# Two of the four attention query projections of a hybrid decoder step computed as one pair of block products

## The chip, the cores and the metric

The kernel is one program on one core of a Trainium2 chip. The metric is the device time of one execution in microseconds (us): the median of three runs is 831.8 us (830.59 to 834.57). One of the executions was profiled, and all durations below are from it.

## What is computed

One inference step of one layer. A prompt of 1024 tokens and 8 sequences of 4 sample tokens each (32 columns) go through a conditioned RMS norm, and the normed rows h are multiplied by one wide matrix w_in, whose columns feed everything else. Cut to what matters here:

```python
h, gate = adaln_in(x, c, w_ada, b_ada, g_norm)
(mq, mk, mv, mi, mf, mo, mz, aq, ak, av, az, gm, ga) = split_in(h @ w_in)
y_m, C, n, m = mlstm_branch(mq, mk, mv, mi, mf, mo, mz, C0, n0, m0, b_i, b_f, g_mn)
q = partial_rope(aq.reshape(B, T, A_HEADS, A_HEAD_DIM), pos)     # 8 query heads, 64 wide
o = attn_prompt(q, k, v, sinks)                                  # window 128, one sink a head
y_a = o.astype(x.dtype) * jax.nn.silu(az)
u = jax.nn.sigmoid(gm) * (y_m @ w_mo) + jax.nn.sigmoid(ga) * (y_a @ w_ao)
x = x + gate * (u @ w_o)
```

The query part aq is 512 columns of w_in: four "query jobs" of 128 columns (two heads each). Each gives a 128 x 1056 result (1024 prompt columns and 32 sample columns).

## The kernel before, in words

All float32 products on TensorE are made of two parts that TensorE multiplies at one column per step: operand = high + low, and high x high, high x low and low x high are summed. So each logical product is three matmuls.

**Plain jobs.** `job` (L569) computes 128 columns of w_in against all 1056 columns of h, in three pieces of 384, 384 and 288 columns (`piece`, L523). Each piece is 8 blocks of the contraction times three matmuls; a job is 72 matmuls. Behind the start, where ak and av are made, eight plain jobs run in this order (L1593 to L1597): aq0 to aq3 (`queries`, L895), mq0, mk0, mv0, mq1 (`head_jobs`). The evacuation of a query piece turns it (`rope`, L769: one shuffle, two products with tables, one sum on VectorE), stores it in qD in DRAM, and for the third piece adds the sample columns into `qpad`.

**Pairs.** The other projections come two at a time (`Pair`, L1366; `block_products`, L1516): two jobs of 128 columns are one 2 x 2 block product with seven block products instead of eight (Winograd's form of Strassen's scheme), each of 4 blocks of the contraction x 3 matmuls of 512 columns: 84 matmuls for a pair. The sums of blocks of h that it needs (t1 to t4) are formed once by `sum_blocks` (L1328): t2, t3 and t4 beside the plain jobs, t1 when they end, since it takes the place of a block that the plain jobs read. The first pair runs its products in the order 1, 6, 2, 7, (1 of the next), 5, 3, 4, so that t1 is wanted late; each later pair in the order 5, 6, 2, 7, (1 of the next), 3, 4. The weights are summed and split two products ahead (`split_ahead`), loaded with `load`, which is emitted at product 5 of the pair before (6 for the first), and the 32 sample columns are a small product of their own (`samples`, `samples_end`), emitted behind product 2 of the pair before (7 for the first). There are 18 pairs (L2011): four `head_in` (mk1 mv1, mq2 mk2, mv2 mq3, mk3 mv3), eight `gate`, two `query_gate`, four `head_gate`.

**Side work.** Everything else is emitted between the matmuls by a planner (`Side`, L113). Its clock `side.now` counts the TensorE time of the products emitted so far. A task is a Python generator: it emits some instructions and yields (lag, banks), and is taken up again when the clock has gone on by the lag and its PSUM banks have been left alone for their hold (a 2.0, b 2.0, o 4.0, and 6.0 us with a "+"). Streams (L266) bound how many tasks run at once: "m" 2 (the gates, then the four mLSTM heads), "a" 5 with 8 us between starts (the prompt attention units, four for each query job, `unit`, L826), "x" (`sum_blocks`), "s" 1 (`sample_attention`, L911, then four sample heads), "g" 1 (`ada_gate`, then `out_weights`). `head_jobs` lowers "a" to 3 when the last plain job starts (L1024) and finishes stream "g" there (L1022). A unit loads queries, keys and values, and 12 us later by the clock does scores (tile sc), then exponentials, transposes (pt), the product with the values (oT) and a store in oD. `head(h)` (L1038) loads q, k and v of one mLSTM head, and 11 us later goes through three groups of chunks.

**What is waited for.** `hook` (L2013) holds a product back by letting the clock run on: product 6 of pair 0 until t2 is formed, product 5 until t1 is, product 6 of a `query_gate` pair until all 16 units are emitted and sample attention is done, product 6 of `head_gate` h until the sample heads are done up to h (they finish in twos).

**Order on the engines.** TensorE executes in the order of emission. The other engines get an order from the framework's scheduler, which may put an instruction ahead of others emitted before it, a DMA issue above all, as soon as its buffer and its source are there by the scheduler's reckoning. All loads and most stores are issued by SyncE in one queue (`issue`, L258), which waits at the head for that DMA's buffer or source. A pool of 50 buffers of 128 x 512 ("half", `ht`, L194) serves nearly all tiles; 24 of them hold t2, t3 and t4 during the pairs. Raw weights have nine buffers (tag "wr"), split weights four and four.

Of the kernel before, what the change touches and what calls it, by code (L numbers as in the profile page):

```python
# [15 lines left out]
ALU = mybir.AluOpType  # L16
# [7 lines left out]
NT = 4  # L24
# [149 lines left out]
def body(tc, a):  # L174
    nc = tc.nc
    with ExitStack() as ctx:
# [17 lines left out]
        def ht(shape, name, dt=F32):  # L194
            return sp.tile(shape, dt, tag="half", bufs=50, name=name)
# [6 lines left out]
        def no_sync(ins, others):  # L202
            for o in others:
                tc.add_manual_dep(ins, o.name, mybir.DependencyInfo(
                    mybir.DependencyClass.NoSync, mybir.DependencyReason.DATA), reason="order of the work")
# [38 lines left out]
        def store(out, in_):  # L244
            due.append((side.now + 8.0, out, in_))
# [8 lines left out]
        def dma(out, in_, late=False):  # L254
            stores(in_.tensor)
            issue(out, in_, late)

        def issue(out, in_, late=False, eng=None):  # L258
            ins = (eng or nc.sync).dma_start(out, in_)  # L259
            ins = getattr(ins, "ins", ins)  # L260
            if late:
                no_sync(ins, free)
                free.clear()
            free.append(ins)
# [645 lines left out]

        def sample_attention():  # L911
            qpad, vns, kTs = at["qpad"], at["vns"], at["kTs"]
            kc, vc = ([ht([128, 4, 128], f"{n}{u}") for u in range(2)] for n in ("kc", "vc"))
            smask = ht([128, 2, WIN + NS], "smask")
            sinkr = cp.tile([128, 1], F32, name="sinkr")
            for u in range(2):
                dma(kc[u], a["cache_k"][:, 4 * u:4 * u + 4])
                dma(vc[u], a["cache_v"][:, 4 * u:4 * u + 4])
            dma(smask, a["smask"])
            dma(sinkr, a["sink_rows"])  # L920
            yield 12.0, "b"
            for u in range(2):
                tq = pb([128, 4, 128], f"kctp{u}")
                for j in range(4):
                    tr(tq[:, j], kc[u][:, j], ident)
                S.copy(kc[u], tq)
                yield 3.0, "b" if u == 0 else "o"
            sc = po([128, 2, WIN + NS], "scs")
            for u in range(2):
                for w in range(4):  # L930
                    b = u * 4 + w
                    qb = qpad[:, b].rearrange("p k g t -> p (k g t)")
                    r = slice(32 * w, 32 * w + 32)
                    mm(sc[r, u, 0:WIN], qb, kc[u][:, w], start=True, stop=True)
                    mm(sc[r, u, WIN:], qb, kTs, start=True, stop=True)
            p = ht([128, 2, WIN + NS], "ps")
            mx = cp.tile([128, 2], F32, name="mxs")
            for u in range(2):
                V.tensor_tensor_reduce(p[:, u], sc[:, u], smask[:, u], 1.0, sinkr, ALU.add, ALU.max,
                                       accum_out=mx[:, u:u + 1])  # L940
            nmx = cp.tile([128, 4], F32, name="nmxs")
            V.tensor_scalar(nmx[:, 0:2], mx, -1.0, None, op0=ALU.mult)
            V.tensor_scalar(nmx[:, 2:4], nmx[:, 0:2], sinkr, None, op0=ALU.add)
            den = cp.tile([128, 2], F32, name="dens")
            for u in range(2):
                S.activation(p[:, u], p[:, u], AF.Exp, bias=nmx[:, u:u + 1], accum_out=den[:, u:u + 1])
            S.activation(nmx[:, 2:4], nmx[:, 2:4], AF.Exp)
            V.tensor_tensor(den, den, nmx[:, 2:4], op=ALU.add)
            V.reciprocal(den, den)
            for u in range(2):  # L950
                V.tensor_scalar(p[:, u], p[:, u], den[:, u:u + 1], None, op0=ALU.mult)
            yield 10.0, "b"
            pt = pb([128, 4, 128], "pts")
            for u in range(2):
                tr(pt[:, u], p[:, u, 0:WIN], ident)
                tr(pt[:NS, 2 + u], p[:, u, WIN:], ident)
            pT = kc[0]
            S.copy(pT[:, 0:2], pt[:, 0:2])
            V.tensor_copy(pT[:NS, 2:4], pt[:NS, 2:4])
            yield 7.0, "o"  # L960
            o = po([128, 2, 128], "os")
            for u in range(2):
                for w in range(4):
                    r = slice(32 * w, 32 * w + 32)
                    mm(o[r, u], pT[:, u, r], vc[u][:, w], start=True, stop=False, share=4)
                for w in range(4):
                    r = slice(32 * w, 32 * w + 32)
                    mm(o[r, u], pT[:NS, 2 + u, r], vns, start=False, stop=True, share=4)
            S.copy(p[:, :, 0:128], o)
            yield 4.0, "b"  # L970
            ot = pb([128, 2, 128], "ost")
            for u in range(2):
                tr(ot[:, u], p[:, u, 0:128], ident)
            for u in range(2):
                v4 = lambda t: t.rearrange("p (w k g t) -> p w k g t", k=2, g=4, t=NT)
                for kv, r in enumerate(half_rows):
                    V.tensor_copy(osm[r, :, 16 * u:16 * u + 16].rearrange("p g (w t) -> p w g t", t=NT), v4(ot[r, u])[:, :, kv])
            samples_done.append("a")


        yhD = [dp.tile([128, SEQ], F32, name=f"yhD{h}") for h in range(NH)]
# [54 lines left out]
        mD = [[dp.tile([128, SEQ], F32, name=f"{n}D{h}") for n in "qkv"] for h in range(NH)]  # L1036

        def head(h):  # L1038
            an, wend, dec, fl = st["an"], st["wend"], st["dec"], st["fl"]
            C = [None]  # L1040
            w_ = {}
# [324 lines left out]
        class Pair:  # L1366
# [12 lines left out]
            def samples(self):  # L1379
                acc = pb([128, 128], "smp")  # L1380
                for k in range(4):
                    for j in range(4):
                        mm(acc[32 * j:32 * j + 32], c32[:, 4 * (j % 2) + k], self.raw[j // 2, j % 2][:, k],
                           start=(k == 0), stop=(k == 3), share=4)
                self.sums = ht([128, 128], "smps")
                S.copy(self.sums, acc)
# [41 lines left out]
        def ahead(self, key, src, th):  # L1428
            self.held[key] = o = ht([128, 512], "ho")
            dma(o, src[:, HALF[th]])  # L1430

        class head_in:
            names = lambda i: paired[i]
            ahead = lambda self, i: None

            def evac(self, c, th, *src):
                n, h = self.names[c]
                scale = float(128 ** -0.5) if n == "mq" else 1.0
                t = ht([128, 512], "mkv")
                if len(src) == 2:  # L1440
                    V.tensor_tensor(t, src[0], src[1], op=ALU.add)
                    src = (t,)
                if len(src) == 1 and (src[0] is not t or n == "mq"):
                    S.activation(t, src[0], AF.Copy, scale=scale)
                issue(mD[h]["mq mk mv".split().index(n)][:, HALF[th]], t, eng=nc.scalar)
                head_part(h, 1)
# [143 lines left out]
                    W = filled(pg, "bw", X, j)  # L1590
                side.tick()

        order += [("ak", 0), ("av", 0)] + [("aq", g) for g in range(4)]  # L1593
        inner = [(n, h) for h in range(NH) for n in ("mq", "mk", "mv")]
        paired = list(zip(inner[4::2], inner[5::2]))
        order += inner[:4]
# [332 lines left out]
        side.add("m", gates(gp, zg, gbias), "")  # L1929
        side.add("a", kv_turn(), "b")  # L1930
        V.on = S.on = False

        gbD, gsD = dp.tile([1, D], F32, name="gbD"), dp.tile([NS, D], F32, name="gsD")

# [73 lines left out]
                    summed("t4", k, b21, t2, ALU.subtract)  # L2008
                    yield 2.4, ""

        pairs = [Pair(head_in, i) for i in range(len(paired))] + [Pair(gate, d) for d in range(KT)] + [Pair(query_gate, i) for i in range(2)] + [Pair(head_gate, h) for h in range(NH)]  # L2011

        def hook(n, i):  # L2013
            if n == 0 and i in (6, 5):
                side.until(lambda: {6: "t2", 5: "t1"}[i] in formed)
            if i == 6:
                if pairs[n].kind is query_gate:
                    side.until(lambda: len(units_done) == 16)
                side.until(lambda: len(samples_done) >= {head_in: 0, gate: 0, query_gate: 1, head_gate: pairs[n].i + 2}[pairs[n].kind])
            if (n, i) == (OUT_WEIGHTS, 6):  # L2020
                side.add("g", out_weights())
            if (n, i) in LOADS:
                side.add("x", att_sums(LOADS.index((n, i))))
            if n == len(pairs) - 1:
                next(att, None)

        OUT_WEIGHTS = 5
        LOADS = [(len(pairs) - 2, 7), (len(pairs) - 1, 5)]
        work = block_products(pairs, hook)
        att = att_products()  # L2030
        side.add("g", ada_gate())
        side.add("x", sum_blocks())
        blocks["t1"] = block(0, 1)
        for g in range(4):
            queries(g)
        side.add("s", sample_attention(), "b")
        for h in range(NH):
            head_jobs(h)

# [337 lines left out]
```

## Time and profile before

| what | us |
|---|---|
| median of three runs | 831.8 |
| the profiled execution's own time | 830.97 |
| its span, first to last instruction | 829.2 |
| TensorE's first matmul starts | 6.45 |
| ak and av jobs (start) | 25.1 to 62.7 |
| eight plain jobs and their side work | 63.8 to 204.6 |
| 18 pairs, first matmul of the first to the last pair's sample matmuls | 204.6 to 617.4 |
| products of w_m_out | 688.4 to 734.5 |

TensorE (PE) is busy for 98% of the span, VectorE (DVE) for 71%, ScalarE (ACT) for 51%. The granted clock is 0.996 on average. In the listings, a group "out<-in" names the tiles written and read; x96 is the number of instructions; times of a matmul include its way through the array, so consecutive starts, not durations, give the rate. "SPq" is the queue of DMA issues.

### The profile page before, as it was taken

The page shows a single profiled execution, that of the slowest core. Times are in us where ns is not written, and L with a number is a line of the kernel's source. Part 1 is how long each engine was busy: PE and PEld are TensorE (multiplying, and loading weights), DVE is VectorE, ACT ScalarE, POOL GpSimd, SP SyncE. Part 2 cuts the span into 40 slices and gives each one's busy share as a digit, 9 for nine tenths or more (in the row PEclk, how much of TensorE's full clock was granted, in tenths as well). Part 3 has the DMA queues.
Part 4 walks back from the last instruction along what each step waited for, and adds up shares of the span by engine and source line. Part 5 has one row for each costly group of instructions (what it writes and reads, how often), then busy time and mean ns, then how long its engine had stood idle before and what let it go on. Part 6 is the DMA issues. An engine that isn't in the chain of part 4 may idle for free. (4 is left out here: it accounts for less than half of the span.)

```text
span 829.2 us, 15039 instructions
## 1 busy us (share of the span) xinstructions
PE 810.1 (98%) x5129; PEld 670.8 (81%) x5129; DVE 592.7 (71%) x1479; ACT 420.6 (51%) x1030; POOL 67.5 (8%) x128
## 2 busy tenths in 40 slices
PE   6999999999999999999899999999999999999996
PEld 3779897888788788888788878888888789987775
DVE  4889886647556456475567786797669988964776
ACT  5664365565474564555455454554446654334343
POOL 0120000000000001000001010000002104250000
PEclk9999999999999999999999999999999999999999
DMA  9997756346435324468756354464336785543533
GB/s 332 379 359 239 200 186 212 118 151 219 141 111 186 118 81 150 139 242 279 256 191 211 105 169 150 147 205 142 103 120 197 228 295 186 191 146 123 202 109 108
DMA packets 106689, 153.96 MB, mean 186 GB/s; under 512 B 20448, under 2 KB 54368, under 8 KB 106580
## 3 DMA queue, kind: packets, MB, share of 16 engines
q1 hardware_dynamic: 100964, 142.25, 52.2%
q10 hardware_dynamic: 4176, 6.56, 2.2%
q0 software_dynamic: 1472, 4.20, 1.4%
q8 instruction: 40, 0.66, 0.3%
q14 instruction: 37, 0.30, 0.1%
HBM read 109.22 MB, written 44.75 MB: 186 GB/s over the span
## 5 line engine op out<-in xcount | busy, mean ns | idle before, releaser
L220 ACT ACTIVATE p<-p,nmx 128x256 f32<-128x256 f32 (+1 forms) x64 | 31.0, 485 | 12.4 <-DVE nmx L220 12.1
L271 PE MATMUL g_aq<-h_h,wh_aq 128*128 128x384 f32 (+1 forms) x96 | 32.2, 336 | 0.0
L271 PE MATMUL g_aq<-h_h,wl_aq 128*128 128x384 f32 (+1 forms) x96 | 30.9, 322 | 0.0
L271 PE MATMUL g_aq<-h_l,wh_aq 128*128 128x384 f32 (+1 forms) x96 | 30.8, 321 | 0.0
L271 PE MATMUL g_w_mo<-ym_l,wh_w_mo 128*128 128x384 f32 (+1 forms) x96 | 30.8, 321 | 0.0
L271 PE MATMUL g_w_mo<-ym_h,wh_w_mo 128*128 128x384 f32 (+1 forms) x96 | 30.8, 321 | 0.0
L271 PE MATMUL g_w_mo<-ym_l,wl_w_mo 128*128 128x384 f32 (+1 forms) x96 | 30.8, 321 | 0.0
L220 DVE CUSTOM_DVE_ANT_0 p<-sc,cst,sink 128x256 f32<-128x256 f32 (+1 forms) x64 | 26.2, 464 | 5.3 <-PE sc L271 5.2
L259 POOL DMA_DIRECT2D oD<-uqv x16 | 8.9, 554 | 183.2 <-ACT uqv L220 161.0
L220 DVE COPY p<-pt 128x512 f32<-128x512 f32 (+1 forms) x16 | 10.5, 656 | 13.6 <-PE pt L276 13.6
L271 PEld LDWEIGHTS g_aq<-h_h,wh_aq 128*128 128x128 f32 x96 | 18.0, 188 | 2.5 <-issue 1.5
L271 PEld LDWEIGHTS g_w_mo<-ym_l,wh_w_mo 128*128 128x128 f32 x96 | 18.0, 188 | 0.0
L271 PEld LDWEIGHTS g_aq<-h_l,wh_aq 128*128 128x128 f32 x96 | 18.0, 188 | 0.0
L271 PEld LDWEIGHTS g_w_mo<-ym_h,wh_w_mo 128*128 128x128 f32 x96 | 18.0, 188 | 0.0
L271 PE MATMUL sc<-ukv,uqv 64*128 64x256 f32 (+1 forms) x128 | 18.0, 390 | 0.0
L271 PEld LDWEIGHTS g_w_mo<-ym_l,wl_w_mo 128*128 128x128 f32 x96 | 18.0, 188 | 0.0
L271 PEld LDWEIGHTS g_aq<-h_h,wl_aq 128*128 128x128 f32 x96 | 18.0, 188 | 0.0
L220 ACT ACTIVATE p<-p,den 128x256 f32<-128x256 f32 (+1 forms) x32 | 14.5, 491 | 5.7 <-DVE den L220 5.6
L220 DVE TENSOR_TENSOR et<-et,S 128x384 f32<-128x384 f32 (+1 forms) x12 | 6.1, 510 | 15.6 <-PE S L271 12.9
L220 ACT ACTIVATE sq<-rows_h 128x512 f32<-128x512 f32 (+2 forms) x14 | 8.2, 582 | 17.8 <-issue 12.0
L271 PE MATMUL g_mq<-h_h,wh_mq 128*128 128x384 f32 (+1 forms) x48 | 16.8, 349 | 0.3 <-ACT mk L220 0.3
L276 PE MATMUL pt<-cst,p 128*128 128x128 f32 x120 | 16.4, 277 | 0.5 <-DVE mx L220 0.5
(2073 smaller groups left out, 2842.4 us busy)
## 6 DMA issues: line engine op xcount, KB each, us to landing
x<-xT SPq DMA_DIRECT2D x16, 256.0 KB, 5.4
early_h<-w_ada SPq DMA_DIRECT2D x8, 512.0 KB, 9.0
adar_ga<-w_ada SPq DMA_DIRECT2D x16, 256.0 KB, 3.9
wr_ga<-w SPq DMA_DIRECT2D x16, 256.0 KB, 2.9
wr_gm<-w SPq DMA_DIRECT2D x16, 256.0 KB, 3.0
taD<-gt SPq DMA_DIRECT2D x16, 256.0 KB, 2.0
tmD<-gt SPq DMA_DIRECT2D x16, 256.0 KB, 5.5
wor<-w_out SPq DMA_DIRECT2D x16, 256.0 KB, 4.9
```

What stands on the lines that cost most here:

```text
L220: ins = f(*args, **kw)
L259: ins = (eng or nc.sync).dma_start(out, in_)
L271: in_order(nc.tensor.matmul(out, lhsT, rhs, start=start, stop=stop, skip_group_check=more))
L276: in_order(nc.tensor.transpose(out, in_, idn))
```

## The change

- The third and fourth query jobs leave the plain jobs and become pair 0, of a new kind `att_in`, ahead of the four `head_in` pairs. Six plain jobs and 19 pairs are left. Its `evac` sums the two parts where there are two, turns the 512 columns (shuffle, two scaled products with tables of their own, a sum), stores them in qD, and adds the four units of a query job when both halves of it are there. Its tables are loaded at product 6 (`ahead`), four of 128 x 512 and a small one.
- Its `samples` writes the sample columns of both jobs into `qpad` and starts sample attention. That first waits until four units are done, bounds the units at once to two while it runs (three afterwards), and loads the cached values later.
- A head waits until the gates are done and t1 is formed.
- While `paced` is set (from the end of the start to the first product of the last pair but one), each DMA that goes through SyncE's queue gets an ordering edge, without a semaphore, to the last TensorE instruction emitted before it.
- `out_weights` starts at pair 8 instead of 5. As the list of pairs has one more at its head, that is two pairs later in the work.

```diff
+        paced = []
+
         def issue(out, in_, late=False, eng=None):
             ins = (eng or nc.sync).dma_start(out, in_)
             ins = getattr(ins, "ins", ins)
+            if eng is None and paced:
+                no_sync(ins, [last["PE"]])
...
         def sample_attention():
             qpad, vns, kTs = at["qpad"], at["vns"], at["kTs"]
-            kc, vc = ([ht([128, 4, 128], f"{n}{u}") for u in range(2)] for n in ("kc", "vc"))
+            while len(units_done) < 4:
+                yield 1.0, ""
+            side.streams["a"]["max"] = 2
+            kc = [ht([128, 4, 128], f"kc{u}") for u in range(2)]
...
+            vc = [ht([128, 4, 128], f"vc{u}") for u in range(2)]
+            for u in range(2):
+                dma(vc[u], a["cache_v"][:, 4 * u:4 * u + 4])
             yield 10.0, "b"
...
             samples_done.append("a")
+            side.streams["a"]["max"] = 3
...
         def head(h):
+            while not st or "t1" not in formed:
+                yield 1.0, ""
...
+        class att_in:
+            names = lambda i: (("aq", 2 * i), ("aq", 2 * i + 1))
+
+            def ahead(self, i):
+                if i == 6:
+                    tables.extend([ht([128, 512], f"turn{th}{j}") for j in range(2)] for th in range(2))
+                    at["turn"] = ht([128, 2, NS], "turns")
+                    dma(at["turn"], a["rope"][:, :, SEQ:T])
+                    for th in range(2):
+                        for j in range(2):
+                            dma(tables[th][j], a["rope"][:, j, HALF[th]])
+
+            def evac(self, c, th, *src):
+                g = 2 * self.i + c
+                x, t = ht([128, 512], "aq"), ht([128, 512], "aqr")
+                if len(src) == 2:
+                    V.tensor_tensor(x, src[0], src[1], op=ALU.add)
+                else:
+                    S.copy(x, src[0])
+                V.stream_shuffle(t, x, shuf)
+                for y, f in zip((x, t), tables[th]):
+                    V.scalar_tensor_tensor(y, y, 0.125, f, op0=ALU.mult, op1=ALU.mult)
+                V.tensor_tensor(x, x, t, op=ALU.add)
+                store(qD[g][:, HALF[th]], x)
+                self.held[c] = self.held.get(c, 0) + 1
+                if self.held[c] == 2:
+                    for b0 in (0, 2, 4, 6):
+                        side.add("a", unit(g, b0))
+
+            def samples(self, o):
+                x, t = sm([128, 2, NS], "gts", 2), sm([128, 2, NS], "gts", 2)
+                S.activation(x, o, AF.Copy, scale=0.125)
+                V.stream_shuffle(t, x, shuf)
+                for y, j in ((x, 0), (t, 1)):
+                    V.tensor_tensor(y, y, at["turn"][:, j:j + 1].to_broadcast((128, 2, NS)), op=ALU.mult)
+                v3 = lambda y, r, c: y[r, c].rearrange("p (b t) -> p b t", t=NT)
+                for c in range(2):
+                    for kv, r in enumerate(half_rows):
+                        V.tensor_tensor(at["qpad"][r, :, kv, 2 * self.i + c], v3(x, r, c), v3(t, r, c), op=ALU.add)
+                side.add("s", sample_attention(), "b")
...
-        order += [("ak", 0), ("av", 0)] + [("aq", g) for g in range(4)]
+        order += [("ak", 0), ("av", 0)] + [("aq", g) for g in range(2)]
...
+        paced.append(True)
...
-        pairs = [Pair(head_in, i) for i in range(len(paired))] + ...
+        pairs = [Pair(att_in, 1)] + [Pair(head_in, i) for i in range(len(paired))] + ...
...
+            if n == len(pairs) - 2:
+                paced.clear()
-        OUT_WEIGHTS = 5
+        OUT_WEIGHTS = 8
...
-        for g in range(4):
+        for g in range(2):
             queries(g)
-        side.add("s", sample_attention(), "b")
```

More of the change, by code (lines that the diff above doesn't have):

```diff
@@ L917, in sample_attention @@
                 dma(kc[u], a["cache_k"][:, 4 * u:4 * u + 4])
-                dma(vc[u], a["cache_v"][:, 4 * u:4 * u + 4])
             dma(smask, a["smask"])
@@ L1430, in ahead @@
             dma(o, src[:, HALF[th]])
+        class att_in:
[35 more added lines that the diff above has]
+                side.add("s", sample_attention(), "b")
+        tables = []
         class head_in:
@@ L2009, in out_weights @@
                     yield 2.4, ""
-        pairs = [Pair(head_in, i) for i in range(len(paired))] + [Pair(gate, d) for d in range(KT)] + [Pair(query_gate, i) for i in range(2)] + [Pair(head_gate, h) for h in range(NH)]
+        pairs = [Pair(att_in, 1)] + [Pair(head_in, i) for i in range(len(paired))] + [Pair(gate, d) for d in range(KT)] + [Pair(query_gate, i) for i in range(2)] + [Pair(head_gate, h) for h in range(NH)]
         def hook(n, i):
@@ L2018, in hook @@
                     side.until(lambda: len(units_done) == 16)
-                side.until(lambda: len(samples_done) >= {head_in: 0, gate: 0, query_gate: 1, head_gate: pairs[n].i + 2}[pairs[n].kind])
+                side.until(lambda: len(samples_done) >= {att_in: 0, head_in: 0, gate: 0, query_gate: 1, head_gate: pairs[n].i + 2}[pairs[n].kind])
             if (n, i) == (OUT_WEIGHTS, 6):
```

## The prediction

> **What bounds the kernel now.** I read the page first: shares, span and clock.
>
> ```profile
> span 829.2 us, 15039 instructions
> PE 810.1 (98%) x5129; PEld 670.8 (81%) x5129; DVE 592.7 (71%) x1479; ACT 420.6 (51%) x1030; POOL 67.5 (8%) x128
> PEclk9999999999999999999999999999999999999999
> ```
>
> TensorE is busy for 810.1 of 829.2 us at nearly the full clock. A busy share can hide waiting, so next the waits of TensorE:
>
> ```profile
> PE xc L271 <- ACT xsq L220: 6.5, 1, 6.5
> PE S L271 <- DVE C L220: 2.3, 1, 2.3
> ...
> PE bw L271 <- ACT bw L220: 0.7, 1, 0.7
> PE pt L276 <- DVE mx L220: 0.5, 1, 0.5
> PE g_mq L271 <- ACT mk L220: 0.3, 1, 0.3
> PE aw L271 <- ACT aw L220: 0.2, 1, 0.2
> ```
>
> Behind the start (xc; the two left out are there too) only 2.3 + 0.7 + 0.5 + 0.3 + 0.2 = 4.0 us is waited for. So the time is the sum of TensorE's issue times, and the change is worth what it takes from that sum, less new waits. The only wait over 1 us also shows what a stall costs beside itself:
>
> ```profile
> 406.80 1.21 PE L271 MATMUL S<-hq,hk 128*128 128x128 f32 x4 [2.26 <-DVE C L220]
> 407.66 0.77 PE L271 MATMUL bw<-t2h,wh_pgate__4792 128*128 128x512 f32 x1
> ...
> 410.32 0.39 PE L271 MATMUL bx<-h_h,wh_pgate__4824 128*128 128x512 f32 x1
> ```
>
> Behind 2.26 us of idle time six 512-column matmuls (one by one in the timeline) take 410.32 - 407.66 = 2.66 us, where six at the rate found below take 1.36: over 1 us more.
>
> **The change: removed.** Two plain jobs leave. Their rate is cleanest where plain jobs run with no side work, in the chain of work:
>
> ```profile
> 688.57 45.94 PE g_w_mo L271 x288
> ```
>
> 288 matmuls of the same mix (384, 384, 288 columns) in 45.94 us are 0.1595 us each, so a job of 72 is 11.48 us and two are **22.97 us**.
>
> **Added.** One pair. Rows of the timeline in a late pair with little beside it:
>
> ```profile
> 530.82 1.08 PE L271 MATMUL smp<-wr_az,c 128*32 128x128 f32 x32
> 531.72 0.62 PE L271 MATMUL sn<-Cs,qd 128*32 128x129 f32 x16
> ...
> 532.60 0.50 PE L271 MATMUL by<-t3h,wh_pquery_gate__6291 128*128 128x512 f32 x1
> 532.94 0.39 PE L271 MATMUL by<-t3l,wh_pquery_gate__6291 128*128 128x512 f32 x1
> ...
> 544.75 0.39 PE L271 MATMUL bz<-h_h,wh_pquery_gate__6436 128*128 128x512 f32 x1
> ...
> 552.91 0.33 PE L271 MATMUL smpo<-cst,smps 128*128 128x64 f32 x2
> 553.17 0.30 PE L271 MATMUL smp<-wr_mo,c 128*32 128x128 f32 x2
> ```
>
> From bz to smpo lie 36 matmuls in 8.16 us: 0.2267 us each, 84 of them 19.04 us. The samples add 531.72 - 530.82 = 0.90 and 553.17 - 552.91 = 0.26, and a return from small float32 matmuls to the wide ones costs 0.34 - 0.23 = 0.11 (532.60 to 532.94). A pair is **20.31 us**. The net on TensorE is 20.31 - 22.97 = **-2.66 us**. Pair 0's two extra copies (bw, by) and their wait of 0.7 us only pass from one pair to another.
>
> The Trainium skill has another price ("TensorE: Matmul & The Clock Gate", Back-to-back issue gap): N / 2.4 + 2.5 ns, so an estimate of 216, 162.5 and 122.5 ns for 512, 384 and 288 columns. By it the two jobs would be 21.5 us and the pair 19.4, a net of -2.1. The rows here, 227 ns for 512, are dearer for each matmul, which favours the form with fewer of them, and they decide.
>
> **Moved.** The units, heads and sample attention keep their TensorE work; only their neighbours change. Each visit among wide matmuls costs that 0.11 us. Eight units with three visits each move; if half of them merge with other visits or no longer do, that is 12 x 0.11 = 1.3 us either way. I take 0.
>
> **Covers.** Pair 0 now starts sooner. How soon, and what must be ready:
>
> ```profile
> 142.07 0.34 PE L271 MATMUL g_mk<-h_h,wh_mk 128*128 128x384 f32 x1
> ...
> 163.62 0.45 PE L271 MATMUL g_mv<-h_h,wh_mv 128*128 128x384 f32 x1
> 144.94 0.60 SPq L259 DMA_DIRECT2D c<-hD  x1
> L220 DVE TENSOR_TENSOR t4l<-x,t4h x4: 669/687/693, 83.9 to 143.0; 128x512 fp32r<-128x512 f32 x4
> ```
>
> Now five jobs are done at 142 and six at 163.6, so pair 0 should start at about 162. t4, the last of t2 to t4, is done at 143.7: about 20 us of cover. The sample columns c are fetched at 144.9, and pair 0's sample product comes a piece into the last plain job, 142 + 24 x 0.17 + visits, about 148: a few us of cover; without it the price is 0 to 3 us, and I take 0. The ends of the side chains:
>
> ```profile
> L271 PE MATMUL oT<-p,uqv x192: 272/273/324, 116.3 to 320.0; 128*64 128x128 f32 x192
> L259 SPq DMA_DIRECT2D ho<-oD x8: 381/388/424, 524.2 to 554.7; - x8
> L220 DVE TENSOR_SCALAR gs<-sty,vec x4: 240/244/251, 517.8 to 580.2; 128x32 f32<-128x32 f32 x4
> 605.40 0.39 PE L271 MATMUL by<-t4h,wh_phead_gate__7097 128*128 128x512 f32 x1
> L259 SPq DMA_DIRECT2D woDt<-wost x8: 319/323/396, 422.1 to 462.4; - x8
> L259 SPq DMA_DIRECT2D wot<-woDt x8: 319/320/624, 675.7 to 708.9; - x8
> ```
>
> Units end at 320 and are first read at 524, so 200 us cover eight late ones, even at 15 us each. The sample heads end at 580.2, and product 6 of the third head gate comes two products behind 605.4, at 611: 31 us of cover for heads that now share the planner's banks with eight units instead of five. The output weights end at 462.4 and are read at 675.7; two pairs later (2 x 25 us) costs nothing. Of these I take 0.
>
> **VectorE** gets work in another place. Durations by shape, and its load by stage:
>
> ```profile
> L220 DVE STREAM_SHUFFLE ropet<-aq 128x384 f32<-128x384 f32 x8 | 4.7, 585 | 0.0
> ...
> L220 DVE TENSOR_TENSOR mkv<-p,bw 128x512 f32<-128x512 f32 x4 | 2.7, 686 | 1.5 <-issue 1.1 <-PE bw L271 0.3
> 64.00:165.00 101.00, 100.66 (x694) 88.00 (x694) 83.25 (x290) 51.63 (x149) 3.79 (x8) 1.00 0.62 190
> 205.00:232.00 27.00, 26.34 (x178) 20.20 (x177) 17.79 (x49) 12.62 (x33) 1.54 (x3) 1.00 0.41 126
> 226.00:251.00 25.00, 25.00 (x157) 20.03 (x159) 13.75 (x44) 17.01 (x52) 0.89 (x3) 1.00 0.30 99
> ```
>
> (The third number is TensorE, the fifth VectorE, with counts in brackets.) An evacuation of pair 0 is a shuffle of 512 (585 x 4/3 = 780 ns, an estimate) and three operations of 686: 2.84 us, four of them 11.3 us, and about as much leaves the plain stage, where VectorE was 82% busy. The sums of the two-part quadrants, 2 x 0.69, stand in for those of mkv. In a stage as the first pair's, 17.79 + 11.3 = 29 us are asked of 27. Between nothing (the turning only delays units, with 200 us of cover) and 4 us (below); I take 0, since the next stage has 11 us of room.
>
> **Paced loads.** The scheduler issues loads early now; behind the change they stand where they were emitted.
>
> ```profile
> 521.32 2.80 SPq L259 DMA_DIRECT2D wr_mo<-w  x2
> ...
> 529.24 3.00 SPq L259 DMA_DIRECT2D wr_mz<-w  x2
> wr_gm<-w SPq DMA_DIRECT2D x16, 256.0 KB, 3.0
> SPq L259 <- ACT gt L220: 43.5, 15, 7.0
> SPq L259 <- DVE wr_ga L220: 14.7, 7, 12.3
> ```
>
> The weights of the pair whose samples start at 553.17 are issued 32 to 21 us ahead of that. They are emitted at product 5 of the pair before, the bz at 544.75: 8.4 us ahead. Four issues of about 0.5 us and 3.0 us to landing need about 5, so 3.4 us remain. The edge has no semaphore, so it changes the queue's order alone; stores that wait at the head for their source (gt, 2.9 us a time) should then stand behind their product too, which frees the queue. A gain of 0 to 3 us (no more is waited for), a loss as in the rival below; I take 0.
>
> **Sum.** 830.97 - 2.66 = 828.3 us for the execution profiled, which lay 0.83 us below the median of 831.8: **829.1 us** for the median. About 0.5% (4.2 us) is what a measurement of this kernel can tell from no change, so this is a gain, but within that bound.
>
> **Rivals.**
>
> *Loads too late (slower).* If the queue is held up for over 3.4 us within the 8.4 us between emission and use, TensorE waits at the sample product of a pair, and likewise at a unit's or a head's first matmul (lags 12 and 11 us). The trace has waits of up to 7.0 and 12.3 us in that queue, against it that they belong to loads hoisted ahead of their buffers. Two waits of 2.5 us leave a load 1.5 us late; with 1 us of slow clock behind it at half of 18 pairs, 9 x 1.3 (some of them too short for the clock) = 12 us: **841 us**. Chance 0.17.
>
> *VectorE binds in pair 0.* Products 5, 3 and 4 each end in an evacuation: 3 x 2.84 + 2 x 0.69 + 3 splits of 0.69 = 12 us against 3 x 12 x 0.2267 = 8.2. It falls 3.8 us behind, and the splits stand only two products (5.4 us) ahead, with a unit between. One stall of about 3 us and 1 us of clock: **833 us**. For it 82% and 29 of 27 above, against it that splits are ready before an evacuation and can go first. Chance 0.12.
>
> *The remaining waits go too.* The order of side work is another one, and the 2.3 us at 406.8 with its slow matmuls, 3.4 us in all, is an accident of the old order: 829.1 - 3.4 = **826 us**. Against it: a new order has accidents of its own. Chance 0.17.
>
> *The change doesn't do what it says* (units late at the query gates, or t2 late) needs the 200 or 20 us above to go; under 0.02, in the first rival.
>
> **Numbers.** Forecast 829.1 with 0.54, its own range 827.2 to 831.5 (the 1.3 us of visits, the runs' scatter, up to 1 us of small waits). The range for 8 in 10 takes in 826 and the lower half of the late loads: 826.0 to 837.5. Faster by over 0.5% (under 827.6): most of the last rival, 0.14, and 0.05 of the forecast, 0.19. Slower (over 836): 0.16 of the first rival and 0.02 of the second, 0.18. Within: 0.63.
>
> **What would show it.** Right: two jobs' g_aq gone (144 matmuls), 84 more of 512 columns, 0.23 us apart, span down by 2 to 3 us, waits behind the start still about 4 us. Late loads: rows "PE smp <- DMA", "PE sc <- DMA", weights issued under 5 us ahead of their samples. VectorE: a wait of PE on wl of the first two pairs, and 9s in its digits there. A wrong cover shows as a wait at pair 0's products 6 or 5, or at the head gates. The forecast is wrong if waits behind the start exceed 8 us or vanish.

## The result, and the profile after

The kernel after takes 845.18 us (median of four runs, 843.66 to 845.86), the kernel before, run beside it, 831.65 (830.59 to 834.57): a ratio of 1.0164, 95% interval 1.0142 to 1.0186. The change makes the kernel slower by 13.5 us, where a gain of 2.7 was forecast. The profiled execution took 845.86 us. The page of after, shares, span and clock:

```profile
span 843.8 us, 14975 instructions
PE 811.9 (96%) x5103; PEld 664.5 (79%) x5103; DVE 594.5 (70%) x1482; ACT 420.8 (50%) x1034; POOL 68.9 (8%) x128
PEclk9999999999999999999999979999999999999998
```

TensorE has 26 instructions fewer and is busy 1.8 us longer, VectorE's work is nearly the same, and one slice in the middle and the last one have a lower clock. TensorE's waits in after (in total, times, longest):

```profile
PE bw L275 <- ACT bw L220: 8.4, 3, 6.3
PE xc L275 <- ACT xsq L220: 6.5, 1, 6.5
PE pt L280 <- DVE mx L220: 4.8, 4, 1.9
PE pt L280 <- DVE gb L220: 1.4, 1, 1.4
PE smpo L275 <- ACT yt L220: 1.0, 1, 1.0
...
PE sc L275 <- DVE p L220: 0.6, 1, 0.6
PE sc L275 <- DMA ukv<-kD: 0.6, 1, 0.6
PE aw L275 <- ACT aw L220: 0.2, 1, 0.2
```

Behind the start (xc) that is 8.4 + 4.8 + 1.4 + 1.0 + 0.6 + 0.6 + 0.2 = 17.0 us, where before had 4.0. Not one of them was in the forecast's sum. The whole difference, from the starts of TensorE's instructions in the two timelines (a wide matmul counted at 226.5, 173.4 or 131.8 ns for 512, 384 or 288 columns, the rest of its time as excess):

| us | before | after | difference |
|---|---|---|---|
| idle, the start's waits included | 11.9 | 24.9 | +13.0 |
| wide matmuls at their usual rate (3030, 2970) | 618.8 | 614.8 | -4.0 |
| their excess: returns from small matmuls | 12.5 | 13.5 | +1.0 |
| their excess: slow clock and the rest | 10.1 | 13.2 | +3.1 |
| small matmuls | 168.4 | 170.1 | +1.7 |
| start of the span to the last start | 821.7 | 836.5 | +14.8 |

The work did fall: -4.0 by the count of matmuls, and 1.2 (the prediction's 0.90 + 0.26) of the small matmuls are the new pair's samples, which makes -2.8. It is buried under waits. Of the 3.1 us of other excess only 1.2 is slow clock (2.5 behind the largest wait, 1.3 in before at 406.8); the last wide matmuls ahead of small ones (52 against 44, about 0.1 us each) are another 1.0. Two stretches of the windows hold most of the waits, after first, then before (TensorE's busy time is the third number, its clock stands ahead of the last two):

```profile
145.00:168.00 23.00, 19.71 (x162) 16.91 (x162) 16.62 (x50) 12.90 (x38) 1.08 (x2) 1.00 0.65 204
463.00:498.00 35.00, 28.63 (x173) 22.59 (x177) 20.61 (x42) 13.42 (x37) 2.78 (x11) 0.85 0.53 172
```

```profile
145.00:168.00 23.00, 23.00 (x195) 20.23 (x194) 14.75 (x57) 13.60 (x44) 1.30 (x3) 1.00 0.36 109
463.00:498.00 35.00, 35.00 (x236) 27.81 (x225) 27.32 (x76) 16.36 (x39) 3.48 (x13) 1.00 0.46 147
```

TensorE stands still for 3.3 us of the first stretch, the end of the plain jobs, and for 6.4 of the second, where its clock falls to 0.85 as well. In before it works through both.

The largest wait, TensorE's rows of after:

```profile
475.35 0.40 PE L275 MATMUL bw<-h_h,wl_pgate__5423 128*128 128x512 f32 x1
...
481.96 0.39 PE L275 MATMUL bz<-h_h,wl_pgate__5509 128*128 128x512 f32 x1
488.70 0.79 PE L275 MATMUL bw<-t2h,wh_pgate__5573 128*128 128x512 f32 x1 [6.35 <-ACT bw L220]
489.29 0.63 PE L275 MATMUL bw<-t2l,wh_pgate__5573 128*128 128x512 f32 x1
489.72 0.63 PE L275 MATMUL bw<-t2h,wl_pgate__5574 128*128 128x512 f32 x1
```

The bank bw holds a finished product since 475.6. VectorE's sum gt<-p,bw empties it, then ScalarE copies bx into it (bw<-bx), and only then can the next pair's product go on in it. VectorE and ScalarE in the same stretch:

```profile
473.64 0.28 DVE L220 COPY sz<-stk 32x128 f32<-32x128 f32 x1 [2.10 <-PE n L275]
...
480.30 0.56 DVE L220 TENSOR_TENSOR Cs<-Cs,sxb 128x387 f32<-128x387 f32 x1
...
481.98 0.69 DVE L220 TENSOR_TENSOR wor<-wor,gb 128x512 f32<-128x512 f32 x1
...
483.81 0.68 DVE L220 TENSOR_TENSOR wost<-wor,wor 128x512 f32<-128x512 f32 x1
...
486.82 0.68 DVE L220 TENSOR_TENSOR gt<-p,bw 128x512 f32<-128x512 f32 x1
...
487.53 0.63 ACT L220 ACTIVATE gt<-gt 128x512 f32<-128x512 f32 x1 [4.75 <-DVE gt L220]
488.07 0.58 ACT L220 COPY bw<-bx 128x512 f32<-128x512 f32 x1
```

VectorE is idle for 2.10 us in front of the first sample head's copy sz, which waits for the last mLSTM head (n), and then works through the sample head (sz to Cs) and the output weights (wor, wost), the head's own operations between them, before it comes to the sum: ready at 475.6, run at 486.8. It is not short of time on average (70%), the sum stands in the wrong place of its queue. Before, the three hardly met: the first sample head starts at 455.8, the last sum of output weights at 461.6, and the last head's n at 470.1. The side chains of after:

```profile
L275 PE MATMUL oT<-p,uqv x192: 272/273/324, 117.2 to 387.9; 128*64 128x128 f32 x192
L220 DVE TENSOR_TENSOR t4l<-x,t4h x4: 668/678/692, 84.0 to 143.6; 128x512 fp32r<-128x512 f32 x4
L261 SPq DMA_DIRECT2D ho<-oD x8: 358/412/1022, 528.3 to 561.4; - x8
L220 DVE TENSOR_SCALAR gs<-sty,vec x4: 242/243/246, 548.4 to 615.5; 128x32 f32<-128x32 f32 x4
L261 SPq DMA_DIRECT2D woDt<-wost x8: 319/323/404, 484.5 to 522.3; - x8
```

Units end at 388 (before 320), the last head's n is at 499.6 (before 470.1), the output weights end at 522 (before 462). All are in time for their readers (the units' at 528.3 in ho<-oD, for one), and each is later than before by 30 to 68 us.

### The profile page after: what moved, and what is told of

Its sections match the earlier page's. It is cut to its first block, busy times and chain, and to the rows that moved or that the text cites. A ratio compares the mean times of both kernels' runs of the same rounds, so it can differ in the third digit from the quotient of the medians.

```text
span 843.8 us, 14975 instructions
## 1 busy us (share of the span) xinstructions
PE 811.9 (96%) x5103; PEld 664.5 (79%) x5103; DVE 594.5 (70%) x1482; ACT 420.8 (50%) x1034; POOL 68.9 (8%) x128
## 5 line engine op out<-in xcount | busy, mean ns | idle before, releaser
L280 PEld LDWEIGHTS pt<-cst,p 128*128 128x128 f32 x120 | 13.5, 141 | 9.3 <-DVE mx L220 4.5
L220 ACT ACTIVATE gt<-gt 128x512 f32<-128x512 f32 (+2 forms) x19 | 10.9, 572 | 15.5 <-DVE gt L220 15.2
L220 DVE SCALAR_TENSOR_TENSOR tgw_mo<-tgw_mo,g_w_mo 128x384 f32<-128x384 f32 (+1 forms) x24 | 12.2, 516 | 6.7 <-PE g_w_mo L275 6.4
L275 PEld LDWEIGHTS sc<-ukv,uqv 64*128 64x128 f32 x128 | 10.7, 186 | 7.5 <-issue 3.6
L275 PE MATMUL g_aq<-h_h,wh_aq 128*128 128x384 f32 (+1 forms) x48 | 16.0, 334 | 0.0
L275 PE MATMUL g_mq<-h_h,wl_mq 128*128 128x384 f32 (+1 forms) x48 | 15.5, 322 | 0.0
```

The costliest lines, as they stand in the source:

```text
L220: ins = f(*args, **kw)
L275: in_order(nc.tensor.matmul(out, lhsT, rhs, start=start, stop=stop, skip_group_check=more))
L280: in_order(nc.tensor.transpose(out, in_, idn))
```

## The experiments

Each ratio is to runs of the kernel before on the same chip beside it (their medians 831.1 to 832.1 us). The theories at first. A: the output weights, two pairs later, meet the first sample head and the last head, and VectorE's backlog holds the sum that frees a bank. B: the ordering edge makes loads late. C: the units that moved beside the pairs cost waits wherever the rest stands. The most direct run on A, the kernel after with the output weights back in their old place in the work (pair 6), gave no time: that order deadlocks.

### The edge and the later weights, each by itself

The kernel after without the ordering edge:

```diff
-        paced.append(True)
```

> The changed kernel without the ordering edge on DMAs; everything else as changed. Theory A: the wait before the bw product at 488.7 stays, 842 to 847 us. Theory B: most of the 13.6 us goes, 830 to 836 us. Theory C: 842 to 847 us, with the waits of pt in the plain stage and beside the pairs still there.

Measured: 843.93 us (842.54 to 845.04), ratio to before 1.0152 [1.0126, 1.0178]. It still waits 15 us behind the start, 5.40 us of it before bw at 488.12, and on no load for longer than in after. **B falls.**

The kernel before with the output weights two pairs later (all else as it was), and the kernel before with the edge alone (the lines on `paced` in the change's diff, and no other):

```diff
-        OUT_WEIGHTS = 5
+        OUT_WEIGHTS = 7
```

> The kernel before with the output weights alone started two pairs later (7 instead of 5), nothing else changed. Theory A: a wait of several us where sample head 0 starts, 835 to 841 us. Theories B and C: 830 to 833 us.

> The kernel before with the ordering edge on DMAs alone (set and cleared at the same places as in the change). Theory A: 829 to 834 us. Theory B: 837 to 845 us. Theory C: 829 to 834 us.

Measured: 829.23 us (827.76 to 831.84), 0.9977 [0.9962, 0.9992], and 829.64 (828.55 to 831.6), 0.9984 [0.9970, 0.9999]. Behind the start no wait of over 2.3 us in either; with the edge the 2.26 us before S at 406.8 are gone. So each part is harmless or better in the old order, and A holds at most together with the later head chain, not for the output weights alone. Nor is it enough that the chains meet: with the weights at 7 the first sample head (454.6 to 475), the first sums of output weights (468.7 to 477) and the last n (469.5) do meet on VectorE, and no bank is waited for there. What counts is what stands ahead of the sum in the queue.

### Four ways at the large wait

A2 is A with that condition, and with a guess at the resource: the sum needs a half buffer, and the lots of output weights hold the last ones. The kernel after with the output weights three pairs later still:

```diff
-        OUT_WEIGHTS = 8
+        OUT_WEIGHTS = 11
```

> The kernel after with the output weights begun three pairs later still (at pair 11 instead of 8), past the last mLSTM head. Theory A2 (the one wait of 6.35 us before bw at 488.70 comes from VectorE's queue: the sum gt takes a half buffer that only the output weights' first lots give back, so it stands behind them, the sample head and the last mLSTM head): the wait goes, with the some 2.6 us of slow clock behind it, so 845.2 - 9 = 836 us, 835 to 839. Theory C (the units that now run beside the pairs bring many small waits wherever the rest stands): the rows pt <- mx (4.8 us) stay, as under A2; if C is the whole cause, another wait of about the same size opens near 490 and the time stays within 843 to 847.

Measured: 836.72 us (836.24 to 837.59), 1.0070 [1.0049, 1.0092]. The wait is gone, the rows pt <- mx (4.8 us) are not. The kernel after with the double lots not fetched a lot ahead, in their old place:

```diff
-                if i + 1 < len(lots):
+                if i + 1 < len(lots) and len(lots[i + 1]) == 1:
                     ahead.append(load(lots[i + 1]))
...
+                if i + 1 < len(lots) and not ahead:
+                    ahead.append(load(lots[i + 1]))
+                    yield 5.0, ""
```

> The kernel after with the output weights in their place, but their double lots no longer fetched one lot ahead, which leaves four half buffers free at the peak. Theory A2: the sum gt finds another buffer and no longer stands behind the output weights' sums; the wait of 6.35 us goes or falls under 2 us, 836 to 839 us. If it is not the buffers but VectorE's sheer load around 480 that holds gt, the wait stays near 6 us and the time at 843 to 846.

Measured: 835.32 us (833.55 to 839.42), 1.0056 [1.0034, 1.0078]. The large wait is gone here too: bw is waited for 1.9 us in all, and the samples that start at 463.0 and 497.8 in after start at 462.5 and 487.4. So the large wait, with what hangs on it, costs about 10 us: 6.35 of wait, 2.5 of slow clock, and about 1 us that was not followed up. The chains still meet in this kernel (sz at 468.5, wost from 477.5, n to 489.9), but the sum runs at 476.9, ahead of the wost.

The kernel after with the gate rows' loads spread over half the time:

```diff
-                    yield 2.0, ""
+                    yield 1.0, ""
```

> The kernel after with the loads of the gate rows spread over half the time (1.0 us a step of the planner instead of 2.0), so that they and their sums gb end earlier in the plain stage. Behind the plain stage's end the kernel after waits 1.40 us on DVE gb, 0.60 and 1.29 us. If these come from the gate rows that end too close to the first pair: about 3 us of waits less and 1 us of slow clock, 841 to 842 us. If the units that follow them are the reason: 844 to 846 us, the same waits under other names.

Measured: **830.02 us** (828.96 to 831.32), 0.9992 [0.9979, 1.0004]: 15 us off, where 3 to 4 were expected. Both large losses are gone at one stroke. TensorE's waits in this kernel:

```profile
PE pt L280 <- DVE mx L220: 1.7, 2, 1.3
PE S L275 <- ACT yt L220: 1.6, 1, 1.6
PE bw L275 <- ACT bw L220: 1.4, 2, 0.7
```

The first half of it was expected. The additions of the second half of the gate rows stood at 143.0 to 148.9 in VectorE's queue of after (four of 0.68 us and a scaling), among the masks of a unit:

```profile
143.03 0.68 DVE L220 TENSOR_TENSOR gb<-ada_ga,gb 9x512 f32<-9x512 f32 x1 [2.15 <-PE ada_ga L275]
...
146.26 0.48 DVE L220 CUSTOM_DVE_ANT_0 p<-sc,cst,sink 128x256 f32<-128x256 f32 x1
...
148.48 1.07 PE L280 MATMUL pt<-cst,p 128*128 128x128 f32 x8 [1.40 <-DVE gb L220]
```

Now they end at 130.7, and the second pair's samples start at 179.5 instead of 184.6: 5.1 us. The second half was not expected. With everything some 5 us earlier, the planner's order near 480 came out another way. The double lots' sums of this kernel and the sample heads' products:

```profile
L220 DVE TENSOR_TENSOR wost<-wor,wor x4: 683/688/693, 463.0 to 505.4; 128x512 f32<-128x512 f32 x4
L220 DVE TENSOR_TENSOR vf<-sz,wm x12: 409/543/549, 479.2 to 566.8; 32x387 f32<-32x387 f32 x8, 32x258 f32<-32x258 f32 x4
```

In after wost began at 483.8, behind the first vf at 474.6; here it is 16 us ahead of it. The crowd is spread out, and no sum stands at its end. That was luck of the order: nothing in the edit aims at it.

The plain stage's end by itself: the kernel after, in which ScalarE copies the sums of gate rows out of the bank before VectorE's additions.

```diff
+                gc = ht([128, 512], f"gc{j}")
+                S.copy(gc, acc)
                 for r in range(0, 128, 32):
-                    V.tensor_tensor(gb, acc[r:r + 9], gb, op=ALU.add)
+                    V.tensor_tensor(gb, gc[r:r + 9], gb, op=ALU.add)
```

> The kernel after with each sum of gate rows copied out of its PSUM bank by ScalarE ahead of the four additions, so that the bank is free without VectorE; everything else in its place. Theory G (the wait of 1.40 us before pt at 148.48 is for the bank that the additions of gb hold, behind a unit's masks): that wait goes, and with it part of the 5 us that the end of the plain stage lost: 840 to 843 us, if the wait of 6.35 us at 488.70 stays; 831 to 836 us if the new order does away with that as well. Rival: VectorE's load is the matter, the four additions still stand in its queue: pt or sc wait as long, 844 to 847 us.

Measured: 844.62 us (842.21 to 845.1), 1.0150 [1.0131, 1.0170]. The wait on gb is gone and the second pair's samples start at 181.9, 2.7 us earlier, so the bank was the matter (theory G). The large wait stayed, and with it the time:

```profile
PE bw L275 <- ACT bw L220: 8.3, 3, 6.3
...
PE pt L280 <- DVE mx L220: 4.1, 4, 1.9
```

The median moved by less than those 2.7 us: behind the unchanged wait of 1.92 us at a pt the clock was now slow for eight matmuls (1.6 us), which in after it was not.

### Late units without a pair

The kernel before with the units of the last two query jobs held back until product 4 of the first pair:

```diff
-                side.add("a", unit(g, b0))
+                if g < 2:
+                    side.add("a", unit(g, b0))
+                else:
+                    kept_units.append((g, b0))
```

> The kernel before, with all its plain jobs, but the units of the query jobs 2 and 3 held back until product 4 of the first pair: late units alone, with no query pair and no later output weights. Theory C (units moved beside the pairs cost time): waits pt <- mx of 3 to 5 us appear and the time rises by 4 to 8 us, to 836 to 839. Theory A2 (the late head chain must meet the output weights): the output weights stand at pair 5, ahead of sample head 0, so no wait of over 3 us on bw; a rise of 0 to 3 us, 831 to 834.

Measured: 841.59 us (840.86 to 843.37), 1.0131 [1.0111, 1.0152], more than C asked for, but by waits of another kind than C named:

```profile
PE bw L271 <- ACT bw L220: 3.7, 2, 3.1
PE sc L271 <- DVE et L220: 3.1, 1, 3.1
...
PE pt L276 <- DVE mx L220: 0.7, 2, 0.4
```

Two waits of 3.1 us, each where late units, heads and output weights share VectorE's queue, and about 3 us of slow clock behind them. Before the first, VectorE's rows:

```profile
364.66 0.69 DVE L220 TENSOR_TENSOR ws<-wr_gm,wr_gm 128x512 f32<-128x512 f32 x1 [2.32 <-DMA wr_gm<-w]
365.26 0.55 DVE L220 TENSOR_TENSOR et<-et,S 128x384 f32<-128x384 f32 x1
```

A sum of weights waits 2.32 us for its load, and behind it stands et, which frees the bank that the unit's scores want. Late units alone, with the work unchanged, cost 10 us. They also put the mLSTM heads back: the last n stands at 500.2 here, 499.6 in after, 470.1 in before, though the change's new conditions on a head are not in this kernel. So C is right that moving the units is dear, and wrong that it is dear by small waits everywhere.

### Is it the change or the draw?

The same edit of the gate rows in the kernel before, to see whether it is simply good for any kernel:

> The kernel before with the loads of the gate rows spread over half the time (1.0 us a step instead of 2.0), the edit that took 15 us off the kernel after. Theory D (the edit mends what the change brought: gate rows that end beside the first pair's preparation, and a later crowd at the output weights): the kernel before has no pair there and only 4 us of waits, so it stays within 829 to 833 us. Rival E (earlier gate rows are simply better in any kernel, and the query pair costs 10 us or more whatever the order): it falls too, to 817 to 825 us.

Measured: 829.13 us (828.43 to 829.47), 0.9972 [0.9959, 0.9985]: 2.8 us, not 15. The edit mends what the change brought (D). Next two kernels made of edits that are shown above: after with the gate rows earlier and the output weights at pair 11, and before with the edge and the output weights two pairs later:

> The kernel after with the gate rows earlier (as in the run at 830.0 us) and the output weights three pairs later. Theory D: the waits of 1.63 us before S at 470 and of VectorE's crowd at 463 to 508 go, the work is 2.7 us less than before's: 826.5 to 829.5 us, under the kernel before. Rival F (each order has accidents of its own, of some us, that no single move removes): another wait appears, 830 to 836 us.

> The kernel before, all plain jobs in place, with the ordering edge of the loads and the output weights two pairs later: the two parts of the change that by themselves gave 829.6 and 829.2 us. If their gains are of different waits they add: 827 to 828.5 us. If both only remove the one wait of 2.26 us before S at 406.8: 829 to 830 us. If the order is a draw (rival F): up to 835 us.

Measured: 828.03 us (826.55 to 829.82), 0.9959 [0.9947, 0.9971], and **827.41** (826.50 to 827.85), 0.9948 [0.9934, 0.9962]: both beat the kernel before, and the second, without the query pair, has the lowest median of the study (the two ranges overlap). It has hardly a wait left (10.8 us idle, 8.4 of it in the start). The best version with the pair has the wide matmuls' 4.0 us less, but 12.2 us idle (1.7 of it at the units' pt beside the pairs), 2.1 more of excess and 0.8 more of small matmuls: the gain is there and is given back.

Then the three edits of order that each gained by itself (edge, output weights at 7, gate rows with 1.0), all in the kernel before:

> The kernel before, all plain jobs in place, with the three small edits of order that gained by themselves: the ordering edge of the loads and the output weights two pairs later (827.4 us together), and the gate rows earlier (829.1 us). If each removes waits of its own: 825.5 to 827 us, the least so far. If an order is a draw (rival F), the third edit may bring a wait back: 828 to 834 us.

Measured: **838.45 us** (838.1 to 839.05), 1.0080 [1.0066, 1.0094], slower than before by 6.4 us, though none of its parts was. Its largest wait behind the start and, in the timeline, how it comes about:

```profile
PE bw L275 <- ACT bw L220: 4.1, 1, 4.1
```

```profile
450.20 0.27 DVE L220 COPY sz<-stk 32x128 f32<-32x128 f32 x1
...
451.77 0.67 DVE L220 TENSOR_TENSOR wor<-wor,gb 128x512 f32<-128x512 f32 x1
...
456.25 0.69 DVE L220 TENSOR_TENSOR gt<-p,bw 128x512 f32<-128x512 f32 x1
...
458.18 0.79 PE L275 MATMUL bw<-t2h,wh_pgate__5362 128*128 128x512 f32 x1 [4.08 <-ACT bw L220]
```

The same three chains, the same sum at the end of the crowd, with none of the change's moved jobs or units, though with its edge and its later weights. The last run gives the buffers of the double lots back in this kernel too, by the edit shown for after:

> The kernel before with the three edits of order (838.4 us, with one wait of 4.08 us before bw at 458), and the double lots of the output weights not fetched one lot ahead. Theory A2 (the evacuation's sum takes a half buffer, and these lots hold the last of them while the last head and the first sample head are at work): the wait of 4.08 us before bw goes as it did in the changed kernel, with its 2 us of slow clock: 829 to 833 us. If the crowd on VectorE is the matter and not the buffers: the wait stays over 3 us, 836 to 839 us.

Measured: 831.07 us (830.29 to 832.36), 0.9994 [0.9983, 1.0004]; the wait is 0.86 us, and 7.4 us are gone. In two kernels, then, the wait goes when the double lots are not fetched ahead. The edit also puts a pause of 5.0 us of the planner's clock behind each late fetch, so the runs don't part the buffers from the places that it moves. Two rows of after do speak for the buffers. The copy sz at 473.64 waits for n although its source stk is written by 467.3; sz takes a half buffer, and n reads two (et, qw). And a sum of the same kind, whose sources come from no DMA, waits for a store out of a half buffer (yt), which no such sum does in before:

```profile
468.79 0.69 DVE L220 TENSOR_TENSOR gt<-p,by 128x512 f32<-128x512 f32 x1 [1.92 <-DMA yhD<-yt]
```

For the sum at 486.82 itself the rows give VectorE's order, not the scheduler's reason for it, so that it lacked a half buffer is likely and not shown.

## Why the prediction was wrong

**The step that failed** is the one on covers, "two pairs later (2 x 25 us) costs nothing. Of these I take 0", together with the 0 taken under Moved. Its working was right as far as it went: the output weights, units and sample heads all end before their readers ask, and no TensorE row waits for one of them. But a cover answers only whether a chain's end is in time. It does not say what the chain holds on its way, its place in VectorE's queue, half buffers, a PSUM bank, nor beside what it now runs. The forecast put nothing on those, with 1.3 us either way for visits as their only bound; they came to 17.0 - 4.0 = 13.0 us of waits, 3.1 of excess beside the returns, and 1.0 of returns.

- **What bounds it**: held. The time is TensorE's issue plus its waits, and the table accounts for 14.8 of the 14.9 us between the two profiled executions.
- **Removed and added, -2.66**: held, as far as a count shows it: -2.8 in after and in the kernels at 830.0 and 828.0 us, by the number of matmuls at their unchanged rates.
- **Moved, 1.3 us either way**: as a price of visits it held roughly (+1.0 on the way back, nearly as much on the way out), as a price of moving it did not (late units alone +10 us).
- **Covers**: t4 at 143.6 (forecast 143.7), no wait for the sample columns, none for t2 or t1 at pair 0's products 6 and 5, units done 140 us ahead of the first read. Right, and beside the point.
- **VectorE**: pair 0's evacuations cost nothing that shows; the 0.66 us before its bw stand in before too, at that kernel's first pair. The rival saw the right engine, but it looked at how much is asked of VectorE in a stage; what counted was the order of its queue, 10 us before pair 0 and 300 behind it.
- **Paced loads**: 0 was right. Without the edge the time is 1.2 us less, with ranges that overlap, and alone in before it gains 1.5.
- **The remaining waits go too**: the 2.26 us did go, and the objection noted there, that a new order has accidents of its own, was the whole result.
- **What would show it wrong**: "if waits behind the start exceed 8 us". They are 17.0.

Each piece with its size: 8.5 to 10 us where the three chains meet with the sum behind them (either edit of the output weights removes it and hardly anything else), 5 us at the plain stage's end (earlier gate rows; 2.7 of them by the bank alone), 3.5 us of waits at units beside the pairs, of which 1.7 stay in the best version, against -2.8 of work and -3.5 for the wait at 406.8 with its slow matmuls. That is some 11 to 12 of the 14.8 us; the rest is waits of about 1 us and visits.

What stays open: what the change's other parts do by themselves (sample attention that waits for four units, the bounds on units at once, the heads' conditions), which no run took alone, and how far the planner's order can be foreseen at all. The edits that left the work as it was moved the time by -17 us (after to its best version) to +10 (late units in before), and three that gained one by one lost together.

## What to carry to other kernels

Where one engine is nearly full and the side work comes from a planner, price a move not only by when the moved chain ends but by which other chains it then overlaps, and look there for an operation on another engine's in-order queue that frees what the full engine wants next. A side task that fetches ahead from a shared pool, or that leaves its sum in a PSUM bank behind other work, is the first thing to move or thin out. A change that saves 0.3% of the work must be tried with a few neighbouring orders, since one draw of the order can be worth far more: up to 17 us here, against 2.7.

## What the runs showed of the hardware

A wait is dearer than its length, but not evenly. Behind the 6.35 us, eleven 512-column matmuls run 0.43 us apart instead of 0.23, 2.5 us in all, and the granted clock from 488.70 to 494.50 is 0.50; behind 3.05, 3.08 and 4.08 us six to nine of them, 1.4 to 1.9 us. A wait of 1.92 us at the same instruction cost nothing in after and 1.6 us in the kernel with the double lots not fetched ahead, where the granted clock from 341 to 347 is 0.72, against 1.00 in after. After, then that kernel:

```profile
341.82 0.66 PE L280 MATMUL pt<-cst,p 128*128 128x128 f32 x4 [1.92 <-DVE mx L220]
...
343.47 0.39 PE L275 MATMUL by<-t4h,wl_pgate__3945 128*128 128x512 f32 x1
343.70 0.40 PE L275 MATMUL by<-t4h,wh_pgate__3944 128*128 128x512 f32 x1
```

```profile
341.03 0.66 PE L280 MATMUL pt<-cst,p 128*128 128x128 f32 x4 [1.92 <-DVE mx L220]
...
342.89 0.63 PE L275 MATMUL by<-t4h,wl_pgate__3945 128*128 128x512 f32 x1
343.31 0.63 PE L275 MATMUL by<-t4h,wh_pgate__3944 128*128 128x512 f32 x1
```

The Trainium skill ("TensorE: Matmul & The Clock Gate", Part 1: The HAM clock gate) has the clock halved by an idle window of about 3.4 us in a count that runs on by itself, and 512 / 1.2 = 426.7 ns a matmul in that state. The 0.43 us agree, and the free-running window would explain why the same wait costs once 0 and once 1.6 us; that 1.92 us already can bring it on does not fit a whole idle window of 3.4 us.
